# Output tiles out of PSUM in two copies of 4 banks in place of three of 3, 3 and 2, and zeros set in 20 parts in place of 32

## Chip, cores and metric

The kernel runs on one core of a Trainium2 chip. The metric is its device time in microseconds (us).

## The reference

```python
x, y: (8, 12, 512, 64) float32
out = np.einsum('bhtc,bhsc->bhts', x, y)      # (8, 12, 512, 512) float32
```

There are 96 products of 512 x 64 by 64 x 512. The inputs are 25.2 MB and the output 100.7 MB, so four fifths of the traffic are stores.

## The kernel before

Twelve groups of inputs are loaded into `slots`, five buffers of 2 MB that loads and output tiles share. ScalarE, VectorE and GpSimd cast the inputs and put them in order (`compress`, `mix`; the four copies of a `mix` from `xk` into `xb` are called xb copies below), VectorE transposes them, and 48 output tiles are made, each of 8 matmuls that fill the 8 banks of PSUM once. Of every four tiles ScalarE copies three out of PSUM and VectorE the fourth. A tile then goes to HBM as one store of 2 MB.

```python
slots = ctx.enter_context(tc.tile_pool(name="slots", bufs=SLOTS))        # SLOTS = 5
tpool = ctx.enter_context(tc.tile_pool(name="tpool", bufs=3))
pm3pool = ctx.enter_context(tc.tile_pool(name="pm3psum", bufs=2, space=bass.MemoryType.PSUM))
pm2pool = ctx.enter_context(tc.tile_pool(name="pm2psum", bufs=1, space=bass.MemoryType.PSUM))
# ... cut: load, compress, mix, transposes ...
def result(o):
    i, h = divmod(o, 2)
    xT, yT = made[i]
    otf = slot()
    ot = otf.rearrange("p (r s) -> p r s", s=S)
    for k, n in ((0, 3), (3, 3), (6, 2)):
        pm = (pm3pool if n == 3 else pm2pool).tile([P, n, S], fp32, name=f"pm{n}")
        for j in range(n):
            nc.tensor.matmul(pm[:, j, :], xT[:, k + j, h, :], yT[:, h * S:(h + 1) * S], start=True, stop=True)
        copy(nc.vector if o % 4 == 3 else nc.scalar, ot[:, k:k + n, :], pm)
    if h == 0 and i + 2 < 2 * NG:
        transposes(i + 2)
    elif h == 1 and FIRST <= i + 4 < 2 * NG:
        mix(i + 4, [nc.scalar if o % 4 == 3 else nc.vector] * 4)
    return lambda: nc.sync.dma_start(ov[i, h], otf)
# ... cut: loads of five groups ...
for k in range(0, K * E * D, 64):                                        # K * E * D = 1024
    nc.vector.memset(zeroed[0][:, k:k + 64], 0.0)
    nc.gpsimd.memset(zeroed[1][:, k:k + 64], 0.0)
# ... cut: groups with their compress and mix; three results (o = 0, 1, 2) are made between them,
#     and their stores are issued after the last load; then results 3 to 47 with a store each
```

## Time and profile before

| | before |
|---|---|
| time, median of the first 3 runs | 302.11 us |
| PE / VectorE / ScalarE busy | 48% / 61% / 74% |
| load and store queue, share of the 16 DMA engines | 98.8% |
| store, issue to landing, median | 20.6 us |
| last store issued, end of the span | 280.0, 300.3 us |

A line of the groups reads: line of the program, engine, operation, what it writes and reads, shapes, count, busy time with the mean of one in ns, and idle time before it with what ended most of that. A line of the timeline reads: start, length, engine, line, operation, names, shapes, count of merged instructions, and in brackets the idle time before with its releaser. PE is TensorE's matmuls, DVE is VectorE, ACT is ScalarE, and SPq is the queue that issues the transfers. Two output tiles of ScalarE in the steady part, from ScalarE's timeline of the kernel before:

```profile
206.30 3.71 ACT L66 ACTIVATE slot<-pm 128x1536 f32<-128x1536 f32 x3 [1.22 <-DMA out_dram<-slot]
211.23 3.71 ACT L66 ACTIVATE slot<-pm 128x1536 f32<-128x1536 f32 x3 [1.22 <-DMA out_dram<-slot]
```

Three copies take 3.71 us, and before each tile ScalarE waits 1.22 us for a store to free a buffer.

### The profile page before, as it was taken

How to read it: one execution, taken by the hardware profiler on the slowest of the kernel's cores; microseconds unless marked ns; L12 is line 12 of the kernel's file. 1: busy time of each engine (PE TensorE's matmuls, PEld its weight loads, DVE VectorE, ACT ScalarE, POOL GpSimd, SP SyncE). 2: the span in 40 equal slices, each digit the busy share in tenths (PEclk: the TensorE clock that was granted, in tenths of full speed). 3: DMA queues.
4: the chain of work that ended last, by engine and by line, in shares of the span. 5: the costliest groups of instructions: out<-in, count | busy, mean ns of one | idle time of the engine just before them, and what ended most of it. 6: DMA issues, size and time to landing. Idle time of an engine off the chain costs nothing.

```text
span 300.3 us, 1412 instructions
## 1 busy us (share of the span) xinstructions
PE 145.4 (48%) x377; PEld 46.5 (15%) x384; DVE 182.6 (61%) x160; ACT 221.3 (74%) x169; POOL 59.1 (20%) x56
## 2 busy tenths in 40 slices
PE   0004044138657484856475656655674655673000
PEld 0001011012212121212121212211121211120000
DVE  1568895989984963947909649289195570603200
ACT  4666599998999779789789697888887977364000
POOL 2899999990000000000000000000000000000000
PEclk9999995676978659567957566779657788577555
DMA  7999999999999999999999999999999999999994
GB/s 281 430 421 421 422 423 420 426 429 440 421 431 436 419 436 434 421 436 432 420 450 423 423 439 423 432 439 421 436 432 423 426 438 423 420 421 441 426 430 205
DMA packets 10377, 125.93 MB, mean 419 GB/s; under 512 B 1152, under 2 KB 1152, under 8 KB 1152
## 3 DMA queue, kind: packets, MB, share of 16 engines
q1 hardware_dynamic: 10368, 125.83, 98.8%
q8 instruction: 3, 0.05, 0.1%
q14 instruction: 6, 0.05, 0.0%
HBM read 25.17 MB, written 100.66 MB: 419 GB/s over the span
## 4 chain that ended last, share of the span: by engine, by line
DMA 53%; ACT 11%; DVE 7%; issue 1%; DVEq 1%; PE 0%; ACTq 0%
DMA out_dram<-slot 53%; ACT slot L66 8%; DVE slot L68 7%; ACT xb L66 2%; ACT xk L83 1%; DVEq L192 1%; PE pm L135 0%; ACT yb L66 0%; DVE yb L68 0%; DVEq L68 0%; ACTq L66 0%
## 5 line engine op out<-in xcount | busy, mean ns | idle before, releaser
L135 PE MATMUL pm<-yT,xT 128*128 128x512 bf16 x377 | 145.4, 524 | 129.7 <-ACT slot L66 74.3
L66 ACT ACTIVATE slot<-pm 128x1536 f32<-128x1536 f32 (+1 forms) x108 | 133.2, 1314 | 37.9 <-DMA out_dram<-slot 27.7
L68 DVE COPY slot<-pm 128x1536 f32<-128x1536 f32 (+1 forms) x36 | 54.6, 1571 | 72.5 <-DMA out_dram<-slot 38.0
L135 PEld LDWEIGHTS <-xT 128*128 128x128 bf16 x384 | 46.5, 121 | 227.7 <-issue 194.0
L116 DVE STREAM_TRANSPOSE xT<-xb 128x1024 uint32<-128x1024 uint32 x24 | 48.8, 2034 | 6.2 <-PE pm L135 4.6
L66 ACT ACTIVATE xb<-xk 32x1024 bf16<-32x1024 bf16 x36 | 48.2, 1338 | 0.8
L68 DVE CAST yb<-slot 64x1024 bf16<-64x1024 f32 x24 | 33.8, 1408 | 17.6 <-DMA slot<-in_y_dram 17.3
L68 POOL COPY xb<-xk 32x1024 bf16<-32x1024 bf16 x24 | 38.5, 1606 | 1.2
L83 ACT ACTIVATE xk<-slot 128x2048 bf16<-128x2048 f32 x12 | 22.9, 1910 | 9.6 <-DMA slot<-in_x_dram 9.5
L68 DVE COPY xb<-xk 32x1024 bf16<-32x1024 bf16 x36 | 26.1, 725 | 0.4
L121 DVE STREAM_TRANSPOSE yT<-yb 128x512 uint32<-128x512 uint32 x24 | 25.1, 1044 | 0.0
L68 POOL CAST yb<-slot 64x1024 bf16<-64x1024 f32 x12 | 19.2, 1601 | 7.4 <-DMA slot<-in_y_dram 6.8
L66 ACT ACTIVATE yb<-slot 64x1024 bf16<-64x1024 f32 x12 | 15.9, 1329 | 3.6 <-DMA slot<-in_y_dram 3.5
L83 ACT ACT_TABLE_LOAD x1 | 1.3, 1283 | 0.7 <-PEq L181 0.7
L149 DVE MEMSET xb<- 128x64 uint32 x16 | 1.2, 112 | 0.8 <-PEq L181 0.8
L150 POOL MEMSET xb<- 128x64 uint32 x16 | 1.4, 151 | 0.3 <-POOLq L181 0.3
L181 POOL MEMSET const-float32-0.0<- 128x1 f32 x1 | 0.1, 98 | 0.2 <-issue 0.2
L181 POOL MEMSET const-float32-1.0<- 128x1 f32 x1 | 0.1, 98 | 0.0
L181 POOL MEMSET const-bfloat16-1.0<- 128x1 bf16 x1 | 0.1, 98 | 0.0
L181 POOL MEMSET const-uint8-127<- 128x1 uint8 x1 | 0.1, 98 | 0.0
## 6 DMA issues: line engine op xcount, KB each, us to landing
out_dram<-slot SPq DMA_DIRECT2D x48, 2048.0 KB, 20.6
slot<-in_x_dram SPq DMA_DIRECT2D x12, 1024.0 KB, 17.5
slot<-in_y_dram SPq DMA_DIRECT2D x12, 1024.0 KB, 19.3
```

Source lines behind the costliest of these rows:

```text
L66: nc.scalar.activation(dst, src, COPY)
L68: engine.tensor_copy(dst, src)
L83: nc.scalar.activation(xk.rearrange("p r c -> p (r c)"), both[:, :R * C], COPY)
L116: nc.vector.transpose(xT.rearrange("p (k r e) -> p k e r", k=K, e=E), xb.rearrange("p (k e c) -> p k e c", k=K, e=E),)
L121: nc.vector.transpose(yT.rearrange("p (r j) -> p j r", r=D), yb.rearrange("p (j c) -> p j c", c=D))
L135: nc.tensor.matmul(pm[:, j, :], xT[:, k + j, h, :], yT[:, h * S:(h + 1) * S], start=True, stop=True)
L149: nc.vector.memset(zeroed[0][:, k:k + 64], 0.0)
L150: nc.gpsimd.memset(zeroed[1][:, k:k + 64], 0.0)
L181: nc = _bacc.Bacc("TRN2", target_bir_lowering=False, num_devices=1)
L192: with _tile.TileContext(nc) as tc:
```

## The change

The intent is fewer, wider instructions: 96 copies in place of 144, so that less fixed cost falls on each element, and 4 memsets in place of 16 on VectorE. PSUM is still held in full, as two tiles of 4 banks.

```diff
-    pm3pool = ctx.enter_context(tc.tile_pool(name="pm3psum", bufs=2, space=bass.MemoryType.PSUM))
-    pm2pool = ctx.enter_context(tc.tile_pool(name="pm2psum", bufs=1, space=bass.MemoryType.PSUM))
+    pmpool = ctx.enter_context(tc.tile_pool(name="pmpsum", bufs=2, space=bass.MemoryType.PSUM))
@@ result
-        for k, n in ((0, 3), (3, 3), (6, 2)):
-            pm = (pm3pool if n == 3 else pm2pool).tile([P, n, S], fp32, name=f"pm{n}")
-            for j in range(n):
+        for k in range(0, K, 4):
+            pm = pmpool.tile([P, 4, S], fp32)
+            for j in range(4):
                 nc.tensor.matmul(
                     pm[:, j, :], xT[:, k + j, h, :], yT[:, h * S:(h + 1) * S], start=True, stop=True
                 )
-            copy(nc.vector if o % 4 == 3 else nc.scalar, ot[:, k:k + n, :], pm)
+            copy(nc.vector if o % 4 == 3 else nc.scalar, ot[:, k:k + 4, :], pm)
@@ zeros
-        for k in range(0, K * E * D, 64):
-            nc.vector.memset(zeroed[0][:, k:k + 64], 0.0)
-            nc.gpsimd.memset(zeroed[1][:, k:k + 64], 0.0)
+        for half, engine, part in ((0, nc.vector, 256), (1, nc.gpsimd, 64)):
+            for k in range(0, K * E * D, part):
+                engine.memset(zeroed[half][:, k:k + part], 0.0)
```

## The prediction

> **What bounds the kernel now.** I read the page first, then the DMA by stretches of 5 us, then the landing times of the stores by window, then the waits, and last the timeline of one output tile. From the page of the kernel before (busy time, slices, queues, the chain, the groups of the two copies out of PSUM):
>
> ```profile
> PE 145.4 (48%) x377; PEld 46.5 (15%) x384; DVE 182.6 (61%) x160; ACT 221.3 (74%) x169; POOL 59.1 (20%) x56
> ...
> DMA  7999999999999999999999999999999999999994
> ...
> q1 hardware_dynamic: 10368, 125.83, 98.8%
> ...
> DMA 53%; ACT 11%; DVE 7%; issue 1%; DVEq 1%; PE 0%; ACTq 0%
> ...
> L66 ACT ACTIVATE slot<-pm 128x1536 f32<-128x1536 f32 (+1 forms) x108 | 133.2, 1314 | 37.9 <-DMA out_dram<-slot 27.7
> L68 DVE COPY slot<-pm 128x1536 f32<-128x1536 f32 (+1 forms) x36 | 54.6, 1571 | 72.5 <-DMA out_dram<-slot 38.0
> ```
>
> No compute engine is above 74%, but the one queue that carries loads and stores keeps the 16 DMA engines 98.8% busy: full in 38 of 40 slices, below that only in the first and the last. The chain gives the copies out of PSUM some 15 points of the span (ACT 8.4, DVE 6.6), and this is the trap. Five buffers go round a loop of "fill, send, wait until landed", and the chain walks that loop. To see whether the fill in it costs anything, I ask whether the DMA engines ever pause while a fill goes on.
>
> Stretches of 5 us (columns: stretch, its length, PE, PEld, DVE, ACT, POOL busy with counts, PE clock, DMA share, GB/s):
>
> ```profile
> 0.00:5.00 5.00, 0.00 (x0) 0.00 (x0) 1.22 (x16) 1.28 (x1) 1.57 (x20) 1.00 0.61 211
> 5.00:10.00 5.00, 0.00 (x0) 0.00 (x0) 1.83 (x2) 3.23 (x2) 1.76 (x1) 1.00 1.01 424
> ...
> 80.00:85.00 5.00, 2.64 (x11) 0.96 (x10) 5.00 (x4) 4.94 (x5) 0.00 (x0) 1.00 0.98 419
> ...
> 190.00:195.00 5.00, 3.13 (x10) 1.03 (x9) 0.00 (x0) 3.79 (x4) 0.00 (x0) 0.82 0.99 423
> ...
> 295.00:300.00 5.00, 0.00 (x0) 0.00 (x0) 0.00 (x0) 0.00 (x0) 0.00 (x0) 0.50 0.27 115
> ```
>
> Of the 58 stretches from 5 to 295 us none shows a DMA share under 0.98. The two at the ends leave 124.3 of the 125.93 MB to the 290 us between: 428.6 GB/s. So the time is the start (the first data flow at about 1 to 2 us), the bytes at that rate, and the tail after the last store. A change to copies can act only by letting the DMA engines run dry.
>
> How far from dry are they? For each store, the time from issue to landing; first of the stores issued from 62 to 75 us, where the reserve is thinnest, then of those from 111 to 200 us:
>
> ```profile
> DMA to landing us min/median/max: 12.5/13.6/14.6
> ...
> DMA to landing us min/median/max: 19.5/20.8/21.1
> ```
>
> One store is 2,097 KB, 4.9 us at 428.6 GB/s. In the steady part a store therefore lands after some 4.2 times its own transfer: about 15 us of queue lie ahead of it. Fill and landing together are 3.7 + 20.8 = 24.5 us, which is five transfers of 4.9 us: the loop closes at the rate of the DMA, and the landing time is what gives. If a fill is 0.1 us shorter, the store waits 0.1 us longer in the queue. At the thinnest place, 12.5 us less its own 4.9 and an allowance of 2 us for starting and finishing (my choice) leaves 5.6 us of reserve.
>
> **What the Trainium skill says.** "DMA: Bandwidth & Descriptors", section "Where 436 GB/s comes from": 16 ports of 256 bits at 850 MHz carry 435.2 GB/s, and for traffic between HBM and SBUF the HBM side binds at about 358. The first half agrees with the 428.6 GB/s here (98.5% of it); the second does not: this core alone moves 20% more than 358, and the measurement decides. "VectorE: DVE Perf Modes", the section on the TRN2 errata, gives a copy out of PSUM as 172 cycles plus one per element at 1.2 GHz on ScalarE, and 120 plus one per element at 0.96 GHz on VectorE. For 1,536 elements that is 1,423 and 1,725 ns; the rows by shape show 1,453 and 1,751. For 1,024 elements, 997 and 1,192; shown are 1,038 and 1,213. It agrees within 4%. The same page, section "Zero memsets can be issued as uint32", says that a memset takes one cycle per element: 66.7 ns for 64 elements, against a row of 112 ns, and against 16 of them in 1.22 us by the timeline, 76 ns apart. "PSUM — Partial Sum Buffer", section "The four PSUM rules", limits a matmul's output to one bank, so 8 banks hold exactly one output tile of 4,096 values, before and after.
>
> **The change part by part.** The listing of the two instruction streams shows the order on each engine unchanged; only the groups of matmuls and the widths of copies and memsets differ.
>
> (a) Copies on ScalarE. Three copies of one tile take 3.71 us from the first start to the last end in the timeline, less than 2 x 1.453 + 1.038 = 3.94, as they overlap at the edges; the spacing of two starts is (3.71 - 1.04)/2 = 1.34 us, that is 1.28 for 1,536 elements at 1.2 GHz and 0.06 fixed. A copy of 2,048 elements then lasts, on the slope between the two rows, 1.453 + 512 x (1.453 - 1.038)/512 = 1.868 us, with a spacing of 1.707 + 0.06 = 1.77. Two take 3.63 us: 0.08 us less per tile, 2.9 us over the 36 tiles of ScalarE. Its busy sum falls from 138.2 to 72 x 1.868 = 134.5, 3.7 us less.
>
> (b) Copies on VectorE. Three take 4.55 us; spacing (4.55 - 1.21)/2 = 1.67 = 1.60 + 0.07. One of 2,048 elements: 1.751 + 0.538 = 2.289; two take 2.20 + 2.29 = 4.49, 0.06 less per tile, 0.7 us over 12 tiles. The busy sum falls from 55.6 to 54.9.
>
> (c) Matmuls. The same 384, but PE gets PSUM back 4 banks at a time. At half clock the weight loads of successive matmuls are 0.43 us apart and one matmul lasts 0.59; PE restarts 0.06 us after the copy that freed its banks. Refilling 4 banks takes 0.06 + 3 x 0.43 + 0.59 = 1.94 us at half clock, about 1.1 at full clock (0.22 apart). Meanwhile the other half is copied in 1.87. So where ScalarE does not wait for a buffer and the clock is halved, it waits some 0.1 us for PE per half, and a tile takes 3.8 to 4.0 us, not 3.63. Before, a refill of 3 banks (0.06 + 2 x 0.43 + 0.59 = 1.51) lay under 2.4 us of other copies. This can cost 0.1 to 0.3 us in some tiles and nothing in others, and eats the gain of (a).
>
> (d) Zeros. VectorE sets 1,024 elements in 4 parts, not 16: at best 1.07 us and 4 gaps of 0.01, instead of 1.22. It then waits 6.1 us for the first load anyway. GpSimd's 16 parts stay. Effect on the end: none.
>
> (e) Sum on the path. A tile's fill changes by -0.1 to +0.3 us; the landing time takes up all of it as long as the reserve of 5.6 us holds. The three consecutive ScalarE tiles at 69 to 80 us, the thinnest place, could come at most 3 x 0.3 = 0.9 us later. In the steady part ScalarE needs at most 3 x 4.0 + 5.42 (four xb copies) = 17.4 us per four tiles, against 4 x 4.9 = 19.6 us of DMA. So 0 us. At the end, the last store is issued near 280.0 us with three more ahead of it, and the end is when the queue is empty: again 0.
>
> **The rivals.** R1, faster: the chain is right, and 48 saved copies pay. At 172 cycles (143 ns) each, that is 6.9 us on paper; by (a) and (b) it is 3.6 us at most, 298.5 us. For it speak the issuing queue's waits, 132 us for ScalarE and 63 us for VectorE; against it, that the DMA engines stay at 0.98 or more while that queue waits: the queue is in the issue of stores, not in their transfer. R2, slower: the coarser handover of PSUM makes ScalarE wait for PE, and DMA runs dry. PE already waits 74.3 us for ScalarE and 29.9 for VectorE; but dry would need a fill above 4.9 us per tile on the mean, or a single lag above 5.6 us. If every one of 48 tiles lost 0.3 us on the path, it would be 14 us, 316 us; half of the early tiles would make 2 to 3 us. R3: the rate of the DMA itself moves a little, as its stretches range from 418 to 449 GB/s; 0.2% of it would be 0.6 us either way, with no part of the change to blame.
>
> **Range and chances.** With no effect on the transfers, the time stays 302.1 us. The three runs before lie within 0.1 us; I widen this for R3 and for the head and tail, to 301.5 to 302.8, a little more upward for R2. Faster by over 2% would be under 296.1 us, when the bytes alone at 428.6 GB/s take 293.8 us and head and tail some 7 more: 1%. Slower by over 2% (over 308.2 us) needs some 6 us of dry DMA: 2%. Within 2%: 97%.
>
> **What would show it.** In the profile after: the queue still at 98 to 99% and 428 GB/s between 5 and 295 us; 72 copies near 1.87 us on ScalarE, 24 near 2.29 on VectorE; two in a row taking 3.6 us in the steady part; landing near 20.8 us, at its smallest 11.5 to 13; last store issued at 279 to 281 us. PE's wait for ScalarE may grow, and ScalarE's wait for PE (5.1 us now) to perhaps 5 to 10. The prediction would be wrong if a stretch of 5 us inside the run fell below 0.95, or if the minimum landing time fell toward 7 us.

## The result

The changed kernel takes 302.0 us (median of 6 runs, 301.59 to 302.08), the kernel before 302.11 us (6 runs, 301.77 to 302.23). A ratio here is the mean time of one kernel's fast runs over that of the other's of the same rounds, so it is not quite the ratio of the medians. It is 0.9995, with a 95% interval of 0.9982 to 1.0008: no difference that can be told from none.

The page of the changed kernel, the same lines as of before:

```profile
PE 143.4 (48%) x384; PEld 46.3 (15%) x384; DVE 180.8 (60%) x136; ACT 219.2 (73%) x133; POOL 59.3 (20%) x56
...
DMA  7999999999999999999999999999999999999994
...
q1 hardware_dynamic: 10368, 125.83, 98.8%
...
DMA 49%; ACT 13%; DVE 5%; issue 4%; PE 1%; DVEq 1%; ACTq 0%
...
L65 ACT ACTIVATE slot<-pm 128x2048 f32<-128x2048 f32 x72 | 131.1, 1876 | 40.0 <-DMA out_dram<-slot 31.6
L67 DVE COPY slot<-pm 128x2048 f32<-128x2048 f32 x24 | 53.8, 2285 | 70.3 <-DMA out_dram<-slot 49.0
```

ScalarE spends 2.1 us less in these copies (133.2 before), and is idle before them for 2.1 us more (37.9 before; of it, for stores to free buffers, 3.9 more than 27.7): what the copies save returns as waiting. The shares of the chain shifted between its links though the time did not, a sign that they are no prices.

The stretches of 5 us, and the landing times of stores issued from 62 to 75 us and from 111 to 200 us:

```profile
0.00:5.00 5.00, 0.00 (x0) 0.00 (x0) 1.09 (x4) 1.28 (x1) 1.57 (x20) 1.00 0.64 211
...
80.00:85.00 5.00, 2.49 (x11) 0.87 (x9) 4.52 (x3) 4.96 (x4) 0.00 (x0) 1.00 0.98 418
...
295.00:300.00 5.00, 0.00 (x0) 0.00 (x0) 0.00 (x0) 0.00 (x0) 0.00 (x0) 0.50 0.27 115
```

```profile
DMA to landing us min/median/max: 12.5/13.1/13.6
...
DMA to landing us min/median/max: 19.5/20.8/21.4
```

The row from 80 us is among the lowest between 5 and 295 us; none has a DMA share under 0.98. The first and the last stretch carry what they carried before, so the 290 us between hold the same 124.3 MB at 428.6 GB/s. ScalarE's timeline for the tiles shown of before:

```profile
206.29 3.65 ACT L65 ACTIVATE slot<-pm 128x2048 f32<-128x2048 f32 x2 [1.31 <-DMA out_dram<-slot]
211.22 3.65 ACT L65 ACTIVATE slot<-pm 128x2048 f32<-128x2048 f32 x2 [1.27 <-DMA out_dram<-slot]
```

A tile's copies are 0.06 us shorter, the wait before them is 0.05 to 0.09 longer, and the tiles start within 0.01 us of before.

Between 69 and 81 us, right after a tile of VectorE, ScalarE waits for no store. Its timeline there, of before and then of after:

```profile
68.96 11.10 ACT L66 ACTIVATE slot<-pm 128x1536 f32<-128x1536 f32 x9 [1.03 <-DVE slot L68]
```

```profile
70.12 1.88 ACT L65 ACTIVATE slot<-pm 128x2048 f32<-128x2048 f32 x1 [2.39 <-PE pm L134]
72.18 8.96 ACT L65 ACTIVATE slot<-pm 128x2048 f32<-128x2048 f32 x5 [0.18 <-PE pm L134]
```

These three tiles end at 80.06 us before and at 81.14 after. Nothing of this reaches the end.

### The profile page after: what moved, and what is told of

Same layout as the page of the kernel before. It is cut to its first block, busy times and chain, and to the rows that moved or that the text cites. A ratio compares the mean times of both kernels' runs of the same rounds, so it can differ in the third digit from the quotient of the medians.

```text
span 300.3 us, 1359 instructions
## 1 busy us (share of the span) xinstructions
PE 143.4 (48%) x384; PEld 46.3 (15%) x384; DVE 180.8 (60%) x136; ACT 219.2 (73%) x133; POOL 59.3 (20%) x56
## 2 busy tenths in 40 slices
DMA packets 10375, 125.92 MB, mean 419 GB/s; under 512 B 1152, under 2 KB 1152, under 8 KB 1152
## 4 chain that ended last, share of the span: by engine, by line
DMA 49%; ACT 13%; DVE 5%; issue 4%; PE 1%; DVEq 1%; ACTq 0%
DMA out_dram<-slot 49%; ACT slot L65 10%; DVE slot L67 4%; ACT xb L65 2%; PE pm L134 1%; DVEq L191 1%; ACT xk L82 1%; DVE yb L67 0%; ACT yb L65 0%; DVE yT L120 0%; DVEq L67 0%; ACTq L65 0%
## 5 line engine op out<-in xcount | busy, mean ns | idle before, releaser
L134 PE MATMUL pm<-yT,xT 128*128 128x512 bf16 x384 | 143.4, 519 | 132.5 <-ACT slot L65 78.1
L65 ACT ACTIVATE slot<-pm 128x2048 f32<-128x2048 f32 x72 | 131.1, 1876 | 40.0 <-DMA out_dram<-slot 31.6
L67 DVE COPY slot<-pm 128x2048 f32<-128x2048 f32 x24 | 53.8, 2285 | 70.3 <-DMA out_dram<-slot 49.0
L67 DVE CAST yb<-slot 64x1024 bf16<-64x1024 f32 x24 | 32.7, 1362 | 19.0 <-DMA slot<-in_y_dram 18.7
L149 DVE MEMSET xb<- 128x256 uint32 x4 | 1.1, 272 | 0.9 <-PEq L180 0.9
```

The costliest lines, as they stand in the source:

```text
L65: nc.scalar.activation(dst, src, COPY)
L67: engine.tensor_copy(dst, src)
L149: engine.memset(zeroed[half][:, k:k + part], 0.0)
```

## The experiments

The theory under test: the DMA queue is always full, the landing time of a store is mostly queueing, and a change of the copies is taken up by it. The rivals: R1, the fill is on the path as the chain of waits has it; R2, the coarser handover of PSUM costs time.

### One part at a time

The first kernel takes only the zeros from the change, the second only the copies.

```diff
 # e1_zeros_only, against the kernel before
-        for k in range(0, K * E * D, 64): ...
+        for half, engine, part in ((0, nc.vector, 256), (1, nc.gpsimd, 64)): ...
 # e2_copies_only, against the kernel before
-        for k, n in ((0, 3), (3, 3), (6, 2)): ...
+        for k in range(0, K, 4): ...
```

> The kernel before with the zeros alone set in 20 parts. My theory (the DMA queue is never dry, so nothing outside it counts): 301.8 to 302.3 us, the memset group on VectorE 1.09 us in place of 1.22, followed by the same wait of about 6.2 us for the first load. Rival (fewer instructions at the start pay): 0.1 us less, which lies within the noise of the runs, so only a difference over 0.3 us would speak for it.

> The kernel before with the two wide copies alone. My theory: 301.8 to 302.3 us, an interval of the ratio that includes 1; a tile on ScalarE still takes 3.65 us in place of 3.71. Rival (the chain of waits is to be taken literally, so 48 saved copies pay 2.9 us): 299 us.

The zeros alone: 302.16 us, ratio 1.0005 (0.9993 to 1.0018). The copies alone: 301.94 us, ratio 0.9998 (0.9986 to 1.0011). In the run with the zeros alone VectorE's timeline shows where the time saved on the memsets goes:

```profile
0.86 1.09 DVE L150 MEMSET xb<- 128x256 uint32 x4 [0.86 <-PEq L181]
8.14 2.47 DVE L68 CAST yb<-slot 64x1024 bf16<-64x1024 f32 x2 [6.19 <-DMA slot<-in_y_dram]
```

The four memsets end at 1.95 us and VectorE waits 6.19 us for the first load. So no gain of one part hides a loss of the other: both are zero within 0.2%, and R1's 2.9 us is excluded.

### Longer fills on purpose

If a shorter fill is worth nothing, a longer one should cost nothing either, until it uses up the reserve. The same bytes of the output tile are written twice, so the results stay right.

```diff
             copy(nc.vector if o % 4 == 3 else nc.scalar, ot[:, k:k + 4, :], pm)
+            if k == 4 and o % 4 != 3:
+                copy(nc.scalar, ot[:, 6:8, :], pm[:, 2:4, :])     # e3: 2 banks more
+                # e4 in its place:  copy(nc.scalar, ot[:, 4:8, :], pm)
```

> The changed kernel, with the last two banks of each ScalarE tile copied a second time, so that the fill is about 0.91 us longer on 36 tiles. My theory (landing time gives): ScalarE then needs 3 x 4.56 + 5.42 = 19.1 us per four tiles, still under the 19.7 us of DMA: 302 to 303 us, landing time in the steady part down by about 0.9 from 20.8 us. Rival (the chain literally): 36 x 0.91 = 33 us more, 335 us.

> The same with all four banks of the second half copied a second time: a fill 1.77 us longer on 36 tiles. My theory: ScalarE needs 3 x 5.42 + 5.42 = 21.7 us per four tiles against 19.7 of DMA, so a lag of 2 us per four tiles builds up over some 8 periods between 90 us and the last of the xb copies, 16 us in all, of which the reserve takes 5 to 6 at the thinnest place: about 10 us more, 306 to 320 us, with a DMA share under 0.95 in some stretches. Rival (the chain literally): 36 x 1.77 = 64 us more, 366 us.

With 2 banks more: 303.78 us, ratio to before 1.0058 (1.0045 to 1.0072). ScalarE is busy 256.0 us in place of 219.2, so 37 us of added copying cost 1.7 us, and R1 is far off; but it is above my range by 0.8 us, and the landing time in the steady part fell to 12.7 us and not by 0.9 to 19.9. The stretches of 5 us show where the 1.7 us went:

```profile
55.00:60.00 5.00, 0.00 (x0) 0.00 (x0) 4.96 (x5) 4.87 (x4) 4.82 (x4) 0.50 0.87 349
60.00:65.00 5.00, 2.57 (x6) 0.80 (x6) 1.84 (x2) 4.95 (x4) 2.94 (x3) 0.50 1.00 339
```

The kernel before moved 421 and 428 GB/s there. The missing 72 and 89 GB/s over 5 us each are 0.81 MB, or 1.9 us at 428.6 GB/s. Less than half of that is time without transfers: the DMA share is 0.87 in the first stretch, but 1.00 in the second, where the DMA engines were busy throughout and moved less. Why they did, no run separates. The issue of the last loads and their landing, of the kernel before and then of this one:

```profile
54.33 0.33 SPq L75 DMA_DIRECT2D slot<-in_x_dram  x1
...
DMA to landing us min/median/max: 6.0/6.0/6.0
```

```profile
56.25 0.33 SPq L74 DMA_DIRECT2D slot<-in_x_dram  x1
...
DMA to landing us min/median/max: 4.7/4.7/4.7
```

This load waits for a buffer which ScalarE empties only after it has copied the output tiles 0 and 1, so two longer fills make it 1.9 us later. Before, it landed 6.0 us after its issue, of which 2.4 are its own 1 MB: with the 1.8 us for starting and finishing that the next run shows, some 1.8 us of queue were left ahead of it. So the thinnest place, after the first loads that find the queue empty, is this load at 54 us and not, as I had predicted, the stores between 62 and 75 us. The change moved it from 54.33 to 54.19 us, to the good side, where it earns nothing. In the steady part ScalarE's four tiles took 19.6 to 19.9 us (starts of the xb copies at 86.37, 106.30, 125.92, 145.56 and 165.47 us), no less than four transfers of 4.9, and 0.5 to 0.8 more than the 19.1 that I had summed, with waits of 0.18 us for PE among it: the queue neither ran dry nor filled up again.

With 4 banks more: 327.49 us, ratio 1.0848 (1.0832 to 1.0865), above my range of 306 to 320, and far under R1's 366. ScalarE's timeline and the landing times of the stores from 111 to 200 us:

```profile
113.74 5.39 ACT L65 ACTIVATE xb<-xk 32x1024 bf16<-32x1024 bf16 x4
119.16 7.32 ACT L65 ACTIVATE slot<-pm 128x2048 f32<-128x2048 f32 x4
126.67 5.56 ACT L65 ACTIVATE slot<-pm 128x2048 f32<-128x2048 f32 x3 [0.18 <-PE pm L134]
132.41 3.79 ACT L65 ACTIVATE slot<-pm 128x2048 f32<-128x2048 f32 x2 [0.18 <-PE pm L134]
136.22 5.40 ACT L65 ACTIVATE xb<-xk 32x1024 bf16<-32x1024 bf16 x4
...
DMA to landing us min/median/max: 6.6/6.7/8.9
```

Four tiles take 22.5 us (136.22 less 113.74), 0.8 more than I had summed, with two waits of 0.18 us for PE among it. Already in this window most stores land after 6.7 us, so nothing is ahead of them. That also measures my allowance for starting and finishing a store: 6.7 less 4.9, or 1.8 us, where I had chosen 2. The last load is issued at 58.00 us, 3.7 us later than before, and at 55 to 60 us the DMA share fell to 0.57. But the reserve was not spent there: from 65 to 110 us the share is 0.99 or more, and the landing times fall only by and by, from 12.4 us or more (stores issued from 60 to 80 us) to some 10.2 (90 to 100 us) and 6.6 (120 to 140 us). Then ScalarE sets the pace. Its 22.5 us less 19.7, or 2.8 us per four tiles, over some nine such groups, come near the 25 us, in part by luck: the last store is issued 36.1 us later than before (316.1 and 280.0 us), and the shorter queue at the end gives 11.1 us of that back (9.2 us from there to the end of the span, in place of 20.3).

### Half the stores

To see what the change is worth where the copies are the bound, both kernels store only the second half of each tile. The result is wrong (half of the output is never written); all other work is the same.

```diff
-        return lambda: nc.sync.dma_start(ov[i, h], otf)
+        return lambda: nc.sync.dma_start(ov[i, h][:, :, K * S // 2:], otf[:, K * S // 2:])
```

> The kernel before with only the second half of every output tile stored (a wrong result on purpose): the store bytes are halved, 75.5 MB in all, about 176 us of DMA at 428.6 GB/s, so the copies, not the DMA, should set the end. Worked out from the trace: 65 us of loads, then 37 tiles at 3 x 3.71 + 5.42 = 16.55 us per four, then 8 tiles at 11.1 per four: about 240 us, range 228 to 255; DMA share near 0.7 after 70 us. Both theories need this run as the base of the next one.

> The changed kernel with the same half stores. If fewer copies pay wherever the copies are the bound (R1's mechanism), it is faster than the half-store kernel before by 28 ScalarE tiles x 0.06 = 1.7 us (0.7%). If the coarser handover of PSUM costs (my step c, R2's mechanism), it is slower by 0.1 to 0.3 us per tile, up to 8 us (3%). I expect the two nearly to cancel: a ratio of 0.99 to 1.01 to the half-store kernel before.

The half-store kernel before takes 250.23 us (250.19 to 250.38), the changed one 255.79 us (255.69 to 255.92). From their ratios to the same runs of the kernel before, 0.8469 over 0.8285, the change makes it 2.2% slower. In both the DMA share is only 0.61 to 0.66 in stretches of 60 us from 70 us on, so the copies are the bound. My expectation of near cancelling was wrong; R2's mechanism has the sign, and its estimate of up to 8 us the size. ScalarE's timeline between two groups of xb copies, of the half-store kernel before and then of the changed one:

```profile
80.09 5.42 ACT L66 ACTIVATE xb<-xk 32x1024 bf16<-32x1024 bf16 x4
85.53 10.91 ACT L66 ACTIVATE slot<-pm 128x1536 f32<-128x1536 f32 x9
96.47 5.45 ACT L66 ACTIVATE xb<-xk 32x1024 bf16<-32x1024 bf16 x4
```

```profile
81.09 5.40 ACT L65 ACTIVATE xb<-xk 32x1024 bf16<-32x1024 bf16 x4
86.52 3.65 ACT L65 ACTIVATE slot<-pm 128x2048 f32<-128x2048 f32 x2
90.40 3.65 ACT L65 ACTIVATE slot<-pm 128x2048 f32<-128x2048 f32 x2 [0.23 <-ACT slot L65]
94.28 3.65 ACT L65 ACTIVATE slot<-pm 128x2048 f32<-128x2048 f32 x2 [0.23 <-ACT slot L65]
97.95 5.43 ACT L65 ACTIVATE xb<-xk 32x1024 bf16<-32x1024 bf16 x4
```

Before, nine copies run without a gap. After, each tile is 0.06 us shorter, but a gap of 0.23 us opens between tiles. The profile puts that wait down to ScalarE itself, which had long been done; the timeline of PE, from the same kernel, has the real one:

```profile
74.13 1.02 PE L134 MATMUL pm<-yT,xT 128*128 128x512 bf16 x4 [0.26 <-ACT slot L65]
...
88.45 3.63 PE L134 MATMUL pm<-yT,xT 128*128 128x512 bf16 x8 [2.31 <-ACT slot L65]
```

At 74 us, at the full clock, four matmuls take 1.02 us, and there are no gaps between ScalarE's tiles near it. At 88 us the clock granted is half and eight take 3.63: by the spacing that the prediction used, the first four end near 90.3 us, just before ScalarE goes on at 90.40. The copy of the other half took only 1.8 us meanwhile. By ScalarE's timeline the 5.6 us of the two spans (248.5 and 254.1) divide so: 1.0 us is there at the first xb copies (80.09 and 81.09), 2.1 us come in the eight groups of four tiles up to 211.32 and 214.41, and 2.5 us after that. At two changes from VectorE to ScalarE the first copy of ScalarE waits 2.31 and 2.75 us for PE, in place of 1.22 and 1.33: 2.5 of the 5.6 us arise there and not in the gaps between ScalarE's tiles.

### Smaller handovers

If the handover is the cause, handing PSUM back 2 banks at a time should undo the loss, although it doubles the number of copies. Built on the changed half-store kernel:

```diff
-    pmpool = ctx.enter_context(tc.tile_pool(name="pmpsum", bufs=2, ...))
+    pmpool = ctx.enter_context(tc.tile_pool(name="pmpsum", bufs=4, ...))
-        for k in range(0, K, 4):
-            pm = pmpool.tile([P, 4, S], fp32)
+        for k in range(0, K, 2):
+            pm = pmpool.tile([P, 2, S], fp32)
```

> The changed kernel with half stores, and with PSUM handed over 2 banks at a time in four copies. If the handover of 4 banks made the half-store kernel slower (255.8 against 250.2 us), 2 banks should undo it although there are twice as many copies: PE's refill is 0.06 + 0.43 + 0.59 = 1.08 us at half clock under 2.8 us of other copies, the copies cost 3 x 0.91 + 1.03 = 3.77 us per tile: 249 to 252.5 us. Rival (wide copies or fewer handovers are good and something else, such as the place in the stream or the clock, made it slow): 255 us or more, since each further copy adds its fixed 0.06 us on 36 tiles.

It takes 249.87 us (249.80 to 249.94). ScalarE's timeline between two groups of xb copies:

```profile
84.63 11.11 ACT L65 ACTIVATE slot<-pm 128x1024 f32<-128x1024 f32 x12
95.76 5.46 ACT L65 ACTIVATE xb<-xk 32x1024 bf16<-32x1024 bf16 x4
```

Twelve copies take 11.11 us, 0.2 more than the nine before, and have no gap; the waits at the two changes from VectorE to ScalarE shrink as well, and the whole is 5.9 us under the kernel with 4 banks. The run was made on another chip, where the kernel before took the same 302.11 us; by their ratios to it, 0.8273 (0.8260 to 0.8285) and 0.8285 (0.8274 to 0.8296), the kernels with 2 banks and with 3, 3 and 2 cannot be told apart. The count of copies therefore does not set the time here, and the size of the handover does.

The clock is a rival: in its profiled run the kernel with 4 banks had a lower mean PE clock (0.807, against 0.895 and 0.882 in the half-store kernels with 3, 3, 2 and with 2 banks), most of it between 30 and 70 us. The other runs speak against it. With 3, 3 and 2 banks the mean clock ranged from 0.808 to 0.895 and the time by 0.2 us; with 4 banks from 0.807 to 0.853 and by 0.23 us. At 0.808 the first took 250.19 us, at 0.807 the second 255.92. Half clock also opens no gap by itself. From 102 to 106 us the half-store kernel before had a granted clock of 0.50, and its nine copies ran on:

```profile
101.95 10.91 ACT L66 ACTIVATE slot<-pm 128x1536 f32<-128x1536 f32 x9
```

### Fewer buffers

With five buffers the queue hides the fill. With two it should not. My first edit skipped buffers by allocating tiles that were never used:

```diff
+        if o > 3 and (o - 3) % 2 == 0:
+            for _ in range(SLOTS - 2):
+                slot()
         otf = slot()
```

> The kernel before, with the output tiles from the fourth on going through two of the five buffers. My theory: fill 3.9 + own transfer 4.9 + about 2 us of start and finish = 10.8 us for two transfers of 9.8, so the queue does run dry: 5.4 us per tile and more where the xb copies hold up ScalarE, 310 to 345 us, with landing times of 6.5 to 8 us. Rival (five buffers are not what keeps the queue full): 302 us.

> The changed kernel with the same two buffers. My theory: with the fill on the path, its 0.06 us per tile counts in part: 0 to 2.7 us less than the two-buffer kernel before, unless ScalarE waits for PE at half clock, which would put it above by up to 5 us. Rival (the change is worth nothing anywhere): equal.

> A look again at the two-buffer kernel before, only to have its trace beside the next runs on the same chip: within 1% of the run of three rounds.

These took 302.03 (ratio 0.9999, 0.9985 to 1.0012), 301.85 (0.9993, 0.9979 to 1.0006) and, in one look, 301.81 us. That looks like the rival's verdict, but it is no verdict at all. The landing times of the stores from 111 to 200 us in the first of them:

```profile
DMA to landing us min/median/max: 19.6/20.8/21.4
```

They are those of five buffers: an unused tile takes no buffer, so the edit did nothing. The three serve only as repeats of the two kernels. The edit that works names the two buffers:

```diff
-        otf = slot()
+        if o < 5:
+            reused[o % 2] = slot()
+        otf = reused[o % 2]
```

> The kernel before, with the output tiles from the fourth on written into two fixed buffers in turn (the earlier two-buffer edit left five in use, as its landing time of 20.8 us shows). My theory: fill 3.9 + landing of a store with an empty queue 6.65 (measured in the run with four banks more) = 10.6 us per two tiles against 9.86 of transfers, 0.37 us lost per tile over 45 tiles: 318 us, range 311 to 326, landing times of 6.5 to 8.5 us. Rival (the number of buffers is not what keeps the queue full): 302 us.

> The changed kernel with the same two buffers. Now the fill lies on the path, and since each fill waits for a store, PE has long refilled PSUM, so the coarser handover costs nothing and the shorter copies pay: 0.06 us per tile over two buffers in turn, 45 x 0.03 = 1.4 us less than the two-buffer kernel before, range 0.5 to 2.8. Rival 1 (the change is worth nothing anywhere): within 0.3 us. Rival 2 (the handover costs here too): slower by 1 to 5 us.

The kernel before takes 333.12 us (332.62 to 334.39; ratio to five buffers 1.1035, 1.1011 to 1.1060), the changed one 331.23 us (329.69 to 331.81; ratio 1.0949, 1.0921 to 1.0978). ScalarE's and the stores' lines of the two-buffer kernel before:

```profile
128.86 3.71 ACT L67 ACTIVATE slot<-pm 128x1536 f32<-128x1536 f32 x3 [2.93 <-DMA out_dram<-slot]
...
DMA to landing us min/median/max: 6.7/6.7/8.3
```

Now a store lands after 6.7 us with nothing ahead of it, nearly every fill waits for a store, and the DMA share falls to 0.84 between 120 and 140 us. Buffers, then, are what keeps the queue full. The size was missed: 31 us and not 16, as four tiles take 22.0 to 23.1 us (xb copies at 114.34, 137.44 and 159.41 us) in place of 21.2. I had added means, while the fills of ScalarE and VectorE differ in length and the stores come at unequal distances; what each of these costs no run separates. And here the change does pay: 1.9 us by the medians, in the range expected, with no run of one kernel inside the spread of the other. The line of the changed kernel for the tile shown above:

```profile
128.24 3.65 ACT L66 ACTIVATE slot<-pm 128x2048 f32<-128x2048 f32 x2 [2.93 <-DMA out_dram<-slot]
```

The copies are 0.06 us shorter and the wait for the buffer is the same. So where a fill is on the path and PE has time to refill PSUM during the wait for a buffer, the shorter copies count; that they alone make the 1.9 us is argued, not tested apart.

## Why the prediction was right

- The DMA bound. Right: the share stays at 0.98 or more, and 428.6 GB/s from 5 to 295 us is the same as before. Two buffers and four more banks, both of which let the queue run dry, cost 31 and 25 us, so the full queue is what made the change free.
- Landing time as the buffer. Right in kind: fills 0.06 us shorter led to waits 0.05 to 0.09 us longer, and 37 us of added copying cost 1.7 us. I stretched it too far for longer fills: once ScalarE is no faster than the DMA, the queue does not fill up again after a loss, and if ScalarE is slower, the lag adds up from tile to tile.
- The thinnest place. Wrong. I looked at stores only; after the start the reserve is smallest at the last load, at 54 us, which landed 6.0 us after issue: some 1.8 us, against 5.8 for the thinnest store (12.5 less 4.9 and 1.8). Nothing came of it, since the change did not delay that load.
- Copies, steps (a) and (b). ScalarE's copies last 1.876 us (predicted 1.868) and a tile 3.65 us (3.63); VectorE's last 2.285 us (2.289) and a tile 4.49 us (4.49). The sums of busy time were not comparable as I wrote them: rows split by shape add up overlapping copies, 138.2 us, while the page's common row gives 133.2 before and 131.1 after.
- Handover, step (c). The mechanism was right, with gaps of 0.23 us in tiles at half clock. In the full kernel it lies under the DMA: the three ScalarE tiles after 69 us end 1.1 us later than before. That this is near the 0.9 of step (e) is luck: nearly all of it comes before the first copy, which waits 2.39 us in place of 1.03 after a tile of VectorE, a place that step (c) had not priced, and not as 0.3 us in each tile. ScalarE's wait for PE over the whole run fell to 3.5 us instead of growing to 5 to 10. The end does not move. That the handover would only eat the gain of (a) was too mild: where copies are the bound the net loss, 5.6 us, is three times the gain of 1.7 us that I had reckoned for (a) there.
- Zeros, step (d). Right: 1.09 us and then a wait of 6.19 us.
- The rivals. R1 is refuted at five buffers by both parts alone and by the longer fills, and its sign holds at two. R2 is refuted at full stores and holds at half stores. The two signs belong to different bounds, and in this kernel neither reaches the end. R3 was not needed: the rate is 428.6 GB/s both times.

## What to carry to other kernels

Before pricing an instruction by its share of the chain of waits, look whether the transfer engines ever pause: where buffers go round a loop, the chain runs through fills that only shorten a queue. Find the thinnest reserve over all transfers, loads too, by comparing each one's landing time with its own transfer time. And when copies out of PSUM are the bound, split them by how soon PE gets banks back rather than by their number: here 4 copies of 2 banks took 249.9 us, copies of 3, 3 and 2 took 250.2 (the two cannot be told apart) and 2 of 4 banks took 255.8.

## What the Trainium skill lacked or had wrong

- "DMA: Bandwidth & Descriptors", on where 436 GB/s comes from, has the HBM side bind transfers between HBM and SBUF at about 358 GB/s. One core alone, with four fifths of its bytes stores, held 428.6 GB/s over 290 us here. The sentence is too general by the page's own account: just before it, under "Measured", one core reaches 425 GB/s when it loads 16 MB, and 358 is given for two cores that stream at once.
- "VectorE: DVE Perf Modes", in the table of its TRN2 errata, gives the length of one copy out of PSUM, and agrees: by an estimate from the table 1,850 ns for 2,048 elements on ScalarE against 1,876 measured, and 2,258 against 2,285 on VectorE. The table leaves out that successive copies overlap, so that a dropped copy saves less than its fixed term (the skill does have the overlap, on other pages): on ScalarE two copies of 1,876 ns took 3.65 us and not 3.75, and dropping one copy of three saved 0.06 us, not the 0.14 us of the table's fixed term.
- "PSUM — Partial Sum Buffer", in its summary of rules for kernel authors, advises to evacuate promptly, but does not say that the size of what is handed back matters: the same 8 banks gave 249.9 and 250.2 us (not told apart) in units of 2 banks and of 3, 3 and 2, and 255.8 us in units of 4, where ScalarE was the bound.
